# A two-layer encoder trunk on one core: the transposition stages between the layers at each piece of the pass over memory, and eight products of zeros at the head

## The chip, the core and the metric

The kernel runs on one core of a Trainium2 chip. The engines that matter here are TensorE (PE in the profile; its loads of the stationary operand are PEld), VectorE (DVE), ScalarE (ACT), GpSimd (POOL) and SyncE (SP, which issues most of the DMAs). Each has a queue of its own, and they meet at semaphores. The metric is the device time of one execution in microseconds, the median of several runs. The time of the kernel before and the profile of one of its executions are below.

## What is computed

The reference is a trunk of two layers over 256 tokens of width 2048, batch 1. Each layer projects its input once, runs three groups of heads side by side (banded softmax attention, gated linear attention, attention into 256 memory tokens), multiplies each group by a SiLU gate, projects the joined groups and normalizes the residual:

```python
def hybrid_layer(x, mem, w_in, rel_table, gate_w, gate_b, gla_norm_g, w_mem_kv, w_out, ln_g, ln_b):
    h = x @ w_in
    ...
    mkv = mem @ w_mem_kv
    mk, mv = jnp.split(mkv, 2, axis=-1)
    ...
    y = jnp.concatenate([y_a * jax.nn.silu(a_z), y_b * jax.nn.silu(b_z), y_m * jax.nn.silu(m_z)], axis=-1)
    out = y @ w_out
    return layer_norm(DEEPNORM_ALPHA * x + out, ln_g, ln_b)
```

Two things matter for the change. `mem @ w_mem_kv` doesn't depend on the layer's input, so the second layer can start with it while the first layer's output is still being normalized. And the normalized output is the input of the next layer's projection: it is needed with the model's width on the partitions, that is transposed.

## The kernel before

**Products.** All large products are of float32 operands that are split in two parts: a high part (a cast on ACT) and a low part (the rest, a subtraction on DVE), with high x high, high x low and low x high added up in PSUM. The functions high (L189) and low (L202) split each weight load, parts (L340) splits an activation. A load is 128 x 1024 floats, 512 KB. The list of loads is laid out by plan (L128) in the order of use; take (L236) hands the next one to the products and lets advance (L214) issue casts three loads ahead, splits two ahead, and DMAs so that at most four raw loads (RAWS) are held. There are four buffers for high parts and three for low parts. A raw buffer is free for its next DMA when its low part is made.

**Who sets the order.** The instructions of PE and of SP stand in the order in which the program emits them. Those of ACT and DVE are placed by a planner, which simulates a timeline; the casts and splits of weights have a high priority there. So a small step on DVE can stand far ahead of its place in the program.

**Work in the gaps.** Small jobs (heads, the normalization) are generators. They are advanced by tick (L92), which the loops over weights call once behind each piece of products. A generator says with `yield n` after how many ticks it is due again; at most two are active, and a tick advances one of them by one step. finish (L108) ticks until the given ones are done, with no products between:

```python
            after = next(g, None)
            if after is not None:
                active.append((g, now[0] + after))
                return
```

**The pass over memory.** A layer starts with `mem @ w_mem_kv` (L723 to L738): 16 pieces, s=0 to s=15, each with one weight load. Pieces 0, 1, 3, 5, 7, 9, 11 and 13 make values (function moving, L291: 12 products), the others keys (function stationary, L282: 16 products). The memory comes in four quarters, each cast and split into an operand tile. Operand tiles (L163) rotate through five buffers, and the four quarters of the layer's transposed input use the same five. Behind each piece stands a tick. After the pass the key sums are added, cast and split (L739 to L743); the tile for them comes from gated (L85), which has two buffers. Then `finish(gens)` (L745) completes what is left of the normalization, and the group of products for the linear attention's queries and keys follows (L757), the first to read the transposed input. Its first half writes PSUM banks 4 and 5.

**The normalization between the layers.** norm_between (L632) is put on the list at the end of layer 0 (L850), so that its steps fall to the ticks of layer 1's pass over memory. It first makes the statistics and normalizes the residual `res` in place (L637 to L642). Then come eight transposition stages, two for each quarter q of the width (L646 to L661), called stage 0 to stage 7 here. A stage takes one of the PSUM banks 4 and 5, the only ones that are free during the pass, transposes four blocks of 128 x 128 on PE (L655), applies the norm's gain and bias with two activations on ACT into a tile from gated() (L658), gives the bank back, and casts and splits the tile into the operand (L660, by way of L341 and L342). The pauses between the steps are 2 after the first quarter's normalization (L644), 3 after all of it (L645), and the one at the end of a stage (L661).

norm_residual (L663) later multiplies `res` by the gain and adds the bias, for the residual of layer 1 (L667, L668); it comes behind the transposes of the same columns.

**The head.** begin (L251) issues the first loads in small parts, and then products of a tile of zeros (L275, L276) whose result is not used; the first true product writes its bank anew. The number is ZEROS (L32).

Of the kernel before, what the change touches and what calls it, by code (L numbers as in the profile page):

```python
# [28 lines left out]

G_MK, G_MV, G_BQK, G_AQ0, G_AK0, G_AQ1, G_AK1, G_MQ, G_BZ, G_AZ0, G_AZ1, G_MZ, G_WO = range(13)  # L30
HI_AHEAD, LO_AHEAD, RAWS = 3, 2, 4
ZEROS = 7  # L32
FILL = 8
AHEAD = 4000

# [8 lines left out]
def hybrid_trunk_kernel(  # L44
# [27 lines left out]
    def nm(s):  # L72
        uid[0] += 1
        return f"{s}_{uid[0]}"

    def mm(o, l, r, start, stop):
        pe.matmul(o, l, r, start=start, stop=stop, skip_group_check=True)  # L77
# [4 lines left out]
    def small(shape, tag, bufs=1):  # L82
        return sm.tile(shape, F32, name=nm(tag), tag=tag, bufs=bufs)

    def gated():  # L85
        return hd.tile([P, 2, T], F32, name=nm("sz"), tag="sz", bufs=2)
# [27 lines left out]
    def banks(n):  # L114
        while len(free) < n:
            yield 1
        return [free.pop(0) for _ in range(n)]

    def release(*bs):
        free.extend(bs)  # L120
# [42 lines left out]
    def operand():  # L163
        return opp.tile([P, 4, 2, T], F32R, name=nm("x"), tag="x")
# [86 lines left out]
    def begin():  # L251
# [22 lines left out]
        at["dma"] = 3  # L274
        for i in range(ZEROS):  # L275
            mm(ps[:, 2 + i % 2], zero[:, :P], zero, True, True)  # L276
# [63 lines left out]
    def parts(hi, lo, src):  # L340
        act.copy(hi, src)  # L341
        dve.tensor_tensor(lo, src, hi.bitcast(F32), op=ALU.subtract)  # L342

    def rsqrt(dst, src, n, epsc):
        v = small([P, n], f"rs_v{n}", 2)
        u = small([P, n], f"rs_u{n}", 2)
        act.activation(u, src, AF.Sqrt, bias=eps[:, 0:1] if epsc == LN_EPS else eps[:, 1:2])
        dve.tensor_scalar(v, src, epsc, -0.5, op0=ALU.add, op1=ALU.mult)
        dve.reciprocal(dst, u)
        dve.tensor_tensor(u, dst, dst, op=ALU.mult)  # L350
        dve.tensor_tensor(u, u, v, op=ALU.mult)
        dve.scalar_tensor_tensor(dst, u, 1.5, dst, op0=ALU.add, op1=ALU.mult)
# [261 lines left out]
    def columns(n):  # L614
        return slice(n * 512, (n + 1) * 512)
# [16 lines left out]
    def norm_between(x):  # L632

        mvt = small([P, 2, 2], "mvt")
        rstd = small([P, 2], "rstd")
        for t in range(2):
            dve.bn_aggr(mvt[:, t], stats[:, t, :4])  # L637
        rsqrt(rstd, mvt[:, :, 1], 2, LN_EPS)
        for q in range(4):
            for t in range(2):  # L640
                r = res[:, t, columns(q)]
                dve.tensor_scalar(r, r, mvt[:, t, 0:1], rstd[:, t:t + 1], op0=ALU.subtract, op1=ALU.mult)  # L642
            if q == 0:
                yield 2  # L644
        yield 3  # L645
        for q in range(4):  # L646
            o = operand()
            x.append(o)
            for j in range(0, 4, 2):
                pt, = yield from banks(1)  # L650
                z = gated()
                for jj in range(2):
                    kt = q * 4 + j + jj
                    for t in range(2):
                        pe.transpose(ps[:, pt, jj * T + t * P:jj * T + (t + 1) * P], res[:, t, kt * P:(kt + 1) * P], ident)  # L655
                for jj in range(2):
                    kt = q * 4 + j + jj
                    act.activation(z[:, jj], ps[:, pt, jj * T:(jj + 1) * T], AF.Identity, bias=lnt[:, 1, kt:kt + 1], scale=lnt[:, 0, kt:kt + 1])  # L658
                release(pt)
                parts(o[:, j:j + 2, 0], o[:, j:j + 2, 1], z)  # L660
                yield 2 if q < 3 else 1  # L661

    def norm_residual(rows):  # L663
        for n, (g, b) in enumerate(rows):
# [50 lines left out]
    for l in range(L):  # L715
# [7 lines left out]
        for s in range(16):  # L723
# [3 lines left out]
            for kk in range(2):  # L727
                kt = p * 2 + kk
                x, j = memq[l][kt // 4], kt % 4
# [47 lines left out]
        def heads():  # L777
            t = hd.tile([P, 4, T], F32, name=nm("qk"), tag="qk", bufs=4)
            for i, a, b in ws_group(l):
                total(t[:, i:i + 2], a, b)  # L780
            return t
# [17 lines left out]
        for half in range(2):  # L799
            values(2 + half)  # L800
            q, k = heads(), heads()
            gens.append([a_head(half * 4 + h, load_bias, bias, q[:, h], k[:, h], asv, yraw[1 + half][:, h]) for h in range(4)])
            waiting.extend(gens[-1])
        q = [hd.tile([P, 4, T], F32R, name=nm("mq"), tag="qk", bufs=4) for _ in range(2)]
# [44 lines left out]
        if not last:  # L849
            gens = [norm_between(xq[l + 1])]  # L850
            waiting.extend(gens)
# [111 lines left out]
```

## Time and profile before

| What | Value |
|---|---|
| Median of 3 runs | 947.04 us |
| Lowest and highest | 946.37 and 947.05 us |
| The profiled execution | 945.37 us |
| Its span, first to last instruction | 943.6 us |
| Mean granted clock of TensorE | 0.993 |
| Moved by DMA | 178.72 MB, mean 189 GB/s |

The profile is of one execution. In its views a row of a timeline has the start in us from the span's start, the busy time, the engine, the line, the operation, the tiles written and read, the shape, how many instructions are merged, and in brackets how long the engine was idle before it and what ended that. A line can be a helper's: L77 is the one function through which nearly all products go, L207 and L200 make the parts of weights, L341 and L342 those of activations. The granted clock is a share of full speed.

### The profile page before, as it was taken

The numbers are of one execution on the slowest core, as the hardware profiler recorded it, in microseconds if no ns is written. First come the engines' busy times: TensorE is split into PE (matmuls) and PEld (weight loads), VectorE is DVE, ScalarE is ACT, GpSimd is POOL, SyncE is SP. The second block draws the span as 40 slices with busy tenths as digits, with TensorE's granted clock in tenths as the row PEclk, the third lists the DMA queues.
The fourth block names the chain that finished last, engine by engine and source line by source line (L and its number), as shares of the span: only waits on it lengthen the run. The fifth ranks groups of instructions, "written<-read, shape, count | busy, mean of one in ns | idle before, by whom it ended". The sixth has DMA issues, their size and how long they took to land.

```text
span 943.6 us, 14238 instructions
## 1 busy us (share of the span) xinstructions
PE 925.7 (98%) x5529; PEld 812.7 (86%) x5529; DVE 588.0 (62%) x779; ACT 502.4 (53%) x721; POOL 16.5 (2%) x38
## 2 busy tenths in 40 slices
PE   8999999999999999999996999999999999999997
PEld 6889998998888888888885899989988888888875
DVE  5674497565566666655688444975655666666566
ACT  5554484474456665443466345755744566654340
POOL 1000000000000010000000000000000000100000
PEclk9999999999999999999998899999999999999999
DMA  8868665555545476655665366654655545665552
GB/s 290 295 197 277 207 202 163 156 175 186 195 157 171 162 221 208 197 191 192 217 205 179 107 178 205 200 164 138 197 183 181 175 157 187 209 207 195 191 172 89
DMA packets 58451, 178.72 MB, mean 189 GB/s; under 512 B 6352, under 2 KB 9488, under 8 KB 58128
## 3 DMA queue, kind: packets, MB, share of 16 engines
q1 hardware_dynamic: 56560, 173.05, 56.3%
q0 software_dynamic: 1536, 4.24, 2.0%
q8 instruction: 43, 0.70, 0.3%
q10 hardware_dynamic: 288, 0.52, 0.2%
q14 instruction: 24, 0.20, 0.1%
HBM read 175.70 MB, written 2.10 MB: 188 GB/s over the span
## 4 chain that ended last, share of the span: by engine, by line
PE 93%; DVE 3%; DMA 2%; issue 1%; ACT 1%; SPq 0%; ACTq 0%; DVEq 0%
PE ps L77 91%; DVE wl L207 1%; DMA room<-w 1%; DMA raw<-w 1%; DMA raw<-memT 1%; PE ps L559 1%; PE ps L597 0%; DVE res L642 0%; DVE res L667 0%; PE ps L655 0%; SPq L272 0%; ACT sz L658 0%; DVE w L207 0%; PE ps L528 0%; SPq L267 0%
## 5 line engine op out<-in xcount | busy, mean ns | idle before, releaser
L207 DVE TENSOR_TENSOR wl<-raw,wh 128x1024 fp32r<-128x1024 f32 (+1 forms) x313 | 366.0, 1171 | 280.7 <-PE ps L77 217.2
L200 ACT CAST wh<-raw 128x1024 fp32r<-128x1024 f32 (+1 forms) x313 | 314.9, 1007 | 333.7 <-PE ps L77 233.6
L77 PE MATMUL ps<-x,wh 128*128 128x512 f32 x1408 | 450.9, 401 | 7.9 <-ACT sz L658 7.7
L77 PEld LDWEIGHTS ps<-x,wl 128*128 128x128 f32 x1408 | 265.3, 188 | 63.4 <-DVE wl L207 1.0
L77 PE MATMUL ps<-wh,x 128*128 128x512 f32 (+1 forms) x1112 | 318.8, 368 | 0.6 <-ACT wh L278 0.6
L77 PE MATMUL ps<-x,wl 128*128 128x256 f32 x1408 | 278.1, 279 | 0.5 <-DVE wl L207 0.5
L77 PEld LDWEIGHTS ps<-x,wh 128*128 128x128 f32 x1408 | 217.5, 190 | 10.8 <-ACT sz L658 8.5
L77 PEld LDWEIGHTS ps<-wh,x 128*128 128x128 f32 x1112 | 204.2, 188 | 24.8 <-ACT wh L278 2.0
L77 PE MATMUL ps<-wl,x 128*128 128x512 f32 (+1 forms) x556 | 204.2, 367 | 1.1 <-DVE wl L207 1.1
L77 PEld LDWEIGHTS ps<-wl,x 128*128 128x128 f32 x556 | 104.3, 188 | 14.8 <-DVE wl L207 2.0
L550 ACT ACTIVATE sc<-sc,mx 128x128 f32<-128x128 f32 (+1 forms) x32 | 14.3, 448 | 19.8 <-DVE mx L548 19.8
L338 DVE SCALAR_TENSOR_TENSOR sz<-ps,sz 128x512 f32<-128x512 f32 x24 | 16.5, 690 | 2.3 <-ACT sz L337 0.3
L619 DVE SCALAR_TENSOR_TENSOR res<-res,ps 128x512 f32<-128x512 f32 x16 | 10.9, 684 | 8.0 <-PE ps L77 8.0
L337 ACT ACTIVATE sz<-ps 128x512 f32<-128x512 f32 x24 | 14.2, 592 | 2.0 <-DVE x L342 1.8
L77 PE MATMUL ps<-w,x 128*128 128x512 f32 (+1 forms) x72 | 14.3, 357 | 0.0
L77 PEld LDWEIGHTS ps<-w,x 128*128 128x128 f32 x72 | 12.0, 189 | 2.2
L406 ACT ACTIVATE sc<-sc 128x512 f32<-128x512 f32 x12 | 7.6, 633 | 11.3 <-DVE sc L404 11.3
L831 DVE TENSOR_TENSOR yr<-sz,yr 128x512 f32<-128x512 f32 x16 | 11.0, 687 | 4.2 <-ACT sz L829 4.2
L829 ACT ACTIVATE sz<-sz 128x512 f32<-128x512 f32 x16 | 10.1, 632 | 6.1 <-DVE sz L338 6.0
L77 PE MATMUL ps<-qk,qk 128*128 128x128 f32 (+1 forms) x64 | 13.1, 327 | 0.0
L77 PE MATMUL ps<-sc,asv 128*128 128x256 f32 (+1 forms) x64 | 13.0, 326 | 0.0
L342 DVE TENSOR_TENSOR x<-yr,x 128x512 fp32r<-128x512 f32 x16 | 10.7, 688 | 3.2 <-ACT x L341 3.1
(171 smaller groups left out, 514.4 us busy)
## 6 DMA issues: line engine op xcount, KB each, us to landing
raw<-w SPq DMA_DIRECT2D x252, 512.0 KB, 3.7
raw<-w SPq DMA_DIRECT2D x64, 388.0 KB, 3.1
bias<-relw SPq DMA_DIRECT2D x16, 192.0 KB, 3.8
res<-xT SPq DMA_DIRECT2D x4, 512.0 KB, 5.8
res<-xn SPq DMA_DIRECT2D x1, 2048.0 KB, 8.2
sc<-ln_g POOLq DMA_DIRECT2D x8, 256.0 KB, 4.4
sc<-ln_b POOLq DMA_DIRECT2D x8, 256.0 KB, 5.9
raw<-memT SPq DMA_DIRECT2D x4, 512.0 KB, 4.8
```

The costliest lines, as they stand in the source:

```text
L77: pe.matmul(o, l, r, start=start, stop=stop, skip_group_check=True)
L200: act.copy(d.hi, d.raw)
L207: dve.tensor_tensor(d.lo, d.raw, d.hi.bitcast(F32), op=ALU.subtract)
L337: act.mul(dst, b, scale)
L338: dve.scalar_tensor_tensor(dst, a, scale, dst, op0=ALU.mult, op1=ALU.add)
L342: dve.tensor_tensor(lo, src, hi.bitcast(F32), op=ALU.subtract)
L406: act.activation(dd, dd, AF.Abs)
L550: act.activation(s[:, own[t]], s[:, own[t]], AF.Exp, bias=mx[:, t:t + 1], accum_out=zs[:, t:t + 1])
L559: pe.transpose(ps[:, pt, i * P:(i + 1) * P], s[:, i * P:(i + 1) * P], ident)
L619: dve.scalar_tensor_tensor(r, r, ALPHA, acc, op0=ALU.mult, op1=ALU.add)
L829: act.activation(sz, sz, AF.Silu)
L831: dve.tensor_tensor(yraw[i][:, j:j + 2], sz, yraw[i][:, j:j + 2], op=ALU.mult)
```

## The change

Two edits. The pause at the end of a transposition stage was 2 ticks for the first three quarters and 1 for the last; it is now 1 tick everywhere, except after the stage (q, j) = (2, 2), the last of the third quarter, where it is 2. And the number of products of zeros at the head goes from 7 to 8.

```diff
-ZEROS = 7
+ZEROS = 8
...
                 release(pt)
                 parts(o[:, j:j + 2, 0], o[:, j:j + 2, 1], z)
-                yield 2 if q < 3 else 1
+                yield 2 if (q, j) == (2, 2) else 1
```

What is computed stays the same.

## The prediction

> **What bounds the kernel now.** I read the page first: who is busy, the granted clock, the chain.
>
> ```profile
> PE 925.7 (98%) x5529; PEld 812.7 (86%) x5529; DVE 588.0 (62%) x779; ACT 502.4 (53%) x721; POOL 16.5 (2%) x38
> PEclk9999999999999999999998899999999999999999
> PE 93%; DVE 3%; DMA 2%; issue 1%; ACT 1%; SPq 0%; ACTq 0%; DVEq 0%
> ```
>
> TensorE (PE) sets the time: busy for 98%, and 93% of the chain. What a change can win is an idle gap of PE, or a stretch at a lower clock; PEclk shows one, slices 22 and 23. So the waits of PE come next: engine and line, what it waited for, us in total, times, longest.
>
> ```profile
> PE ps L77 <- ACT sz L658: 7.7, 2, 6.0
> PE ps L77 <- DVE wl L207: 1.7, 3, 0.6
> ```
>
> Nearly all of it hangs on L658, the gain-and-bias activations of norm_between. The timeline of PE around slices 22 and 23, then a stretch of it (us, busy time and count, clock, DMA):
>
> ```profile
> 506.12 0.63 PE L77 MATMUL ps<-x,wh 128*128 128x512 f32 x2
> ...
> 508.92 1.03 PE L655 MATMUL ps<-ident,res 128*128 128x128 f32 x8
> 510.90 0.66 PE L655 MATMUL ps<-ident,res 128*128 128x128 f32 x4 [0.95 <-ACT sz L658]
> 517.58 0.80 PE L77 MATMUL ps<-x,wh 128*128 128x512 f32 x1 [6.03 <-ACT sz L658]
> 520.07 0.80 PE L77 MATMUL ps<-x,wh 128*128 128x512 f32 x1 [1.69 <-ACT sz L658]
> ...
> 524.48 0.62 PE L77 MATMUL ps<-x,wh 128*128 128x512 f32 x2
> ```
> ```profile
> 517.00:524.40 7.40, 5.13 (x16) 0.53 0.00 0
> ```
>
> Piece s=15, the last of the pass over layer 1's memory, runs from 506.12 to 508.92: 16 products in 2.80 us. Then come the last three of the eight transposition stages (8 and 4 transposes), with waits of 0.95, 6.03 and 1.69 us, and the first 16 products of the next group (the stretch's x16) end only at 524.48, at a granted clock of 0.53. Why 6 us? The other engines between:
>
> ```profile
> 512.12 0.68 DVE L338 SCALAR_TENSOR_TENSOR sz<-ps,sz 128x512 f32<-128x512 f32 x1
> 515.73 0.68 DVE L342 TENSOR_TENSOR mk<-sz,mk 128x512 fp32r<-128x512 f32 x1
> 516.51 1.02 ACT L658 ACTIVATE sz<-ps,lnt 128x256 f32<-128x256 f32 x2 [0.67 <-DVE mk L342]
> 518.99 1.02 ACT L658 ACTIVATE sz<-ps,lnt 128x256 f32<-128x256 f32 x2 [0.30 <-DVE x L342]
> ```
>
> The stages of the last quarter (q=3) run in finish(gens), behind the two key sums of L739 to L743. Both take their tile from gated(), which has two buffers. So stage 7's activations wait until the key sum has been added, cast and split (512.12 to 516.41), and the next product group, which writes banks 4 and 5 (first=4), waits until those activations have emptied the banks.
>
> **The change part by part.** First, the order. norm_between starts at the tick of s=0 and pauses 2 and 3, so its first stage falls to the tick of s=5, before and after. Before, with a pause of 2 the next fall to s=7, 9, 11, 13, 15, and two are left to finish(gens). After, with 1 they fall to s=5, 6, 7, 8, 9, 10; (2,2) pauses 2; the last two fall to s=12 and s=13. finish(gens) then finds nothing to do. The pause serves a buffer: the operand of q=3 takes over that of the memory's third quarter, last read by PE in s=12. The operand of q=2 takes over the second quarter's, last read in s=8, and is wanted at s=9. So neither adds a wait on PE beyond program order.
>
> Second, what a stage costs PE wherever it stands:
>
> ```profile
> 478.98 0.60 PE L655 MATMUL ps<-ident,res 128*128 128x128 f32 x4
> 479.33 0.71 PE L77 MATMUL ps<-x,wh 128*128 128x512 f32 x2
> ...
> 482.20 0.63 PE L77 MATMUL ps<-wh,x 128*128 128x512 f32 x2
> ...
> 484.96 0.60 PE L655 MATMUL ps<-ident,res 128*128 128x128 f32 x4
> 485.31 0.71 PE L77 MATMUL ps<-x,wh 128*128 128x512 f32 x2
> ```
>
> Four transposes take 0.35 us (484.96 to 485.31), and the piece behind them 2.87 us (479.33 to 482.20) against 2.80 for s=15: together 0.42. Three more stages ahead of 508.92 move the end of s=15 to 508.92 + 3 x 0.42 = 510.18. The next 16 products at full pace end at 510.18 + 2.80 = 512.98, instead of 524.48. **Gross gain: 11.50 us**: the three waits (8.67), and the rest the slow clock. Does it reach the end? The waits of PE from 520 us on (its first row, the 1.7 at 520.07, left out), and of all engines:
>
> ```profile
> PE ps L77 <- DVE wl L207: 0.5, 1, 0.5
> PE ps L77 <- ACT row L683: 0.3, 1, 0.3
> ```
> ```profile
> ACT wh L200 <- PE ps L77: 233.6, 157, 3.8
> ```
>
> Past the 1.7 that goes, PE loses 0.8 us more, and the casts ahead of it wait mostly for PE itself. So all of it should arrive.
>
> Third, what the denser stages cost. The stretch from s=5 to s=13 has spare time, but not everywhere. The casts of weights from 476 to 509 us as a group (count, busy us, mean ns, idle before), then the timelines of ScalarE (ACT) and VectorE (DVE):
>
> ```profile
> L200 ACT CAST wh<-raw 128x1024 fp32r<-128x1024 f32 x13 | 13.6, 1049 | 12.3 <-DMA raw<-w 9.5 <-PE ps L77 2.8
> ```
> ```profile
> 483.20 1.05 ACT L200 CAST wh<-raw 128x1024 fp32r<-128x1024 f32 x1 [1.06 <-DMA raw<-w]
> 484.15 1.01 ACT L658 ACTIVATE sz<-ps,lnt 128x256 f32<-128x256 f32 x2
> 485.72 1.04 ACT L200 CAST wh<-raw 128x1024 fp32r<-128x1024 f32 x1
> ```
> ```profile
> 485.85 0.69 DVE L342 TENSOR_TENSOR x<-sz,x 128x512 fp32r<-128x512 f32 x1 [0.34 <-ACT x L341]
> 488.89 1.22 DVE L207 TENSOR_TENSOR wl<-raw,wh 128x1024 fp32r<-128x1024 f32 x1
> ```
>
> A stage takes ACT from 484.15 to 485.72, 1.57 us, and DVE 0.69. It issues no DMA. From 484.15 on ACT has eight stages (12.6), the casts of the seven later loads of the pass (the fourth memory quarter among them) and of the first of the next group (8 x 0.95 = 7.6, by the start-to-start times), and the values' cast (about 1, as large as the weights' at 1049 ns): 21.2 us, done at 505.3 if it never waits. PE needs banks 4 and 5 at 510.18: 4.9 us of slack. ACT waited 9.5 us for weight DMAs here; much of the added 4.7 us (three stages) falls into such waits, and that is its cover. DVE gets 3 x 0.69 = 2.1 us.
>
> The exposed place is the start. The first stage's transposes ended at 479.58 (the row at 478.98); its activations started at 484.15, behind a cast that waited for its DMA: ACT took its queue in order. The stage of s=6 now stands behind it, ahead of casts that fed DVE splits with little to spare: the one at 488.89 ends at 490.1, and PE uses it in s=10, two pieces and a stage after 485.31, about 491.3: 1.2 us. A stage put ahead of those casts delays them by 1.57 us and PE by only 0.42; against the 1.2 that is just even (1.57 - 0.42 - 1.2 = -0.05), so some tenths may show in one or two places. The same holds for the third stage, which may find its bank still full. I bound this new waiting from below at -0.62 (the weight wait of PE just ahead of the first stage, shown below, disappears) and from above at 3 x 1.57 = 4.7, three stages' ACT work wholly on the path. **I take 1.0**, nearest to the 0.95 us bank wait, the only wait of that kind shown. If the DMA waits that hide ACT's work were gone, it would be the 4.7.
>
> A rule speaks against packing stages so closely. The Trainium skill, page "TensorE: Matmul & The Clock Gate", section "A second HAM failure mode: psum-queue depth-cycling", reports a kernel that cycled through PSUM banks, idled briefly between groups of products and had its clock go up and down. By it the sum would be that of the last rival below. Here the trace speaks against it for gaps under 1 us: the stretch with a 0.62 wait keeps clock 1.00, as does all of s=6 to s=13 (us, busy of PE, PEld, DVE, ACT, POOL, clock, DMA), and only the 6.03 wait is followed by 0.53.
>
> ```profile
> 476.59 0.50 PE L77 MATMUL ps<-wl,x 128*128 128x512 f32 x1 [0.62 <-DVE wl L207]
> ```
> ```profile
> 476.00:479.00 3.00, 2.41 (x11) 1.96 (x12) 3.00 (x4) 0.64 (x1) 0.00 (x0) 1.00 0.39 116
> 478.98:502.90 23.92, 23.92 (x130) 20.33 (x129) 17.93 (x22) 16.19 (x23) 0.64 (x2) 1.00 0.76 248
> ```
>
> Fourth, the eighth product of zeros.
>
> ```profile
> 1.51 3.35 PE L77 MATMUL ps<-wh 128*128 128x512 f32 x7 [1.51 <-DVE wh L248]
> 4.83 0.84 PE L77 MATMUL ps<-wh,x 128*128 128x512 f32 x2
> 7.22 0.73 PE L77 MATMUL ps<-wh,x 128*128 128x512 f32 x2 [0.62 <-ACT wh L278]
> ```
>
> Seven take 3.35 us; taking one's 0.80 (the row at 517.58) for the last leaves (3.35 - 0.80) / 6 = 0.43 start to start. The eighth starts at about 4.49, and the first true product moves from 4.83 to 4.92 at most. 0.62 us of waiting at 7.22 for a cast behind a DMA covers that, and covers equally what the first products might gain by a better clock. I take 0; without the cover it would cost 0.1 to 0.43.
>
> **Sum.** 11.5 - 1.0 - 0 = 10.5 us. The profiled execution took 945.37 us, 943.6 of it span; by it the time would be 934.9. It lies 1.67 below the median of the runs, 947.04, which is what is predicted: 947.04 - 10.5 = **936.5 us**.
>
> **The rivals.**
> *ACT and the raw buffers fall behind* (0.14). Four raw buffers are refilled only after DVE's split, so a late stage delays a cast, the split, the next DMA. For it: those DMA waits of 9.5 us. Against: 4.9 us of slack at the end. Price 4.7: 947.04 - 11.5 + 4.7 = 940.2.
> *The group still waits* (0.05): the last stage's activations, queued behind the values' cast and the key sums, release bank 5 late. It takes over 4.9 us of lag; I price it at half of the 6.03 wait: 936.5 + 3.0 = 939.5.
> *No change* (0.02): the wait at 517.58 belongs to something other than these stages, and comes back whole: 947. Against: both activations end just ahead of both products (517.53, 520.01).
> *Slower* (0.04): the bank waits repeat at every stage and the clock falls as it did after 517. Place: s=6 to s=13, 23.92 us and three stages, 25.2 us. At 0.53 they take 25.2 x (1/0.53 - 1) = 22.3 us more: 947.04 - 11.5 + 22.3 = 957.8. It decides from half of the stretch on (11.5 us). For it: two stages back to back cost 0.95. Against: a bank is now wanted again only two pieces, 5.6 us, later.
>
> **How the numbers follow.** The forecast, 0.75, covers 934.3 (947.04 - 11.5 - 0.62 and some half us of measurement) to 939. The first rival reaches past 940.2; range 934.3 to 941.0. A measurement of this kernel tells about 0.2% from no change, 1.9 us, so the first three cases are faster: 0.94, less 0.01 for a tail of the first rival. Faster 0.93, same 0.03, slower 0.04.
>
> **What would show it.** Right: the 7.7 of PE on L658 gone or under 1.5; transposes after s=5, 6, 7, 8, 9, 10, 12, 13; the next group's products right behind s=15 at clock 1.00; slices 22 and 23 at 9; PE busy nearer 99%. ACT's waits for weight DMAs in the pass shorter by some us. Wrong: new PE waits on wl L207, wh L200 or L658 at L655 between 482 and 505 us that sum to over 3 us; a clock below 0.9 there; a wait in front of the second half of the next group, for the key sums; a start moved by more than 0.2 us at 12 us.

## The result, and the profile after

The changed kernel took 933.83 us (median of 4 runs, 933.71 to 934.99), the kernel before 946.7 us (median of 4 runs in the same comparison, 945.1 to 947.05). The ratio, of the means of these runs, is 0.987, with a 95% interval of 0.9853 to 0.9887. The forecast was 936.5 us in a range of 934.3 to 941.0. The sign and the cause were right. The gain was larger than forecast: 933.83 itself lies half a microsecond below the range, and the ratio applied to the 947.04 us that the prediction started from gives 934.7, just inside it.

The page after the change, in the parts that were shown of before: the busy times, the granted clock by slice, the chain.

```profile
PE 923.4 (99%) x5530; PEld 812.0 (87%) x5530; DVE 587.3 (63%) x779; ACT 502.0 (54%) x721; POOL 16.5 (2%) x38
PEclk9999999999999999999999999999999999999999
PE 96%; DMA 1%; DVE 1%; SPq 0%; issue 0%; ACT 0%; ACTq 0%; DVEq 0%
```

PE's busy time hardly moved (925.7 to 923.4 us), but the span fell from 943.6 to 931.9: what went is idle time and a stretch at low clock. Slices 22 and 23 of the clock are at 9. The waits of PE (what it waited for, us in total, times, longest):

```profile
PE ps L77 <- DVE wl L207: 1.6, 3, 0.7
PE ps L77 <- DVE wh L248: 1.5, 1, 1.5
PE ps L77 <- ACT row L683: 0.3, 1, 0.3
```

The 7.7 us for L658 and the 0.9 us at L655 are gone, and nothing took their place. The timeline of PE around the end of the pass, and two stretches of it (us, busy times with counts, clock, DMA):

```profile
503.83 0.60 PE L655 MATMUL ps<-ident,res 128*128 128x128 f32 x4
504.19 0.71 PE L77 MATMUL ps<-x,wh 128*128 128x512 f32 x2
...
509.85 0.63 PE L77 MATMUL ps<-x,wh 128*128 128x512 f32 x2
...
512.63 0.63 PE L77 MATMUL ps<-x,wh 128*128 128x512 f32 x2
```
```profile
478.50:503.80 25.30, 25.30 (x141) 21.68 (x140) 21.33 (x27) 20.48 (x31) 0.64 (x2) 1.00 0.69 218
503.80:520.00 16.20, 16.20 (x95) 14.17 (x94) 15.29 (x19) 11.04 (x15) 0.00 (x0) 1.00 0.70 199
```

The last stage's transposes stand behind s=13 (503.83). Piece s=15 ends at 509.85, the next group follows without a gap, and its first 16 products end at 512.63 where they ended at 524.48. From the first stage to the next group PE is busy for all of both stretches, at clock 1.00, while ACT is busy for 20.48 of 25.30 us (81%).

To compare kernels without the head of the program, whose length differs a little from one execution to the next, I use one length below: **the pass**, from the start of the first stage's transposes (L655) to the start of the next transposes at L372, some way into layer 1's projections. Before and after:

```profile
580.03 0.38 PE L372 MATMUL ps<-ident,asv 128*16 128x128 f32 x2
```
```profile
478.54 0.60 PE L655 MATMUL ps<-ident,res 128*128 128x128 f32 x4
...
568.17 0.38 PE L372 MATMUL ps<-ident,asv 128*16 128x128 f32 x2
```

Before it was 580.03 - 478.98 = 101.05 us, after 568.17 - 478.54 = 89.63: **11.42 us less, where the prediction's gross gain was 11.50**. The 0.44 us by which 478.54 is earlier than 478.98 come from the head and from one wait ahead of the first stage, and other executions of these kernels have them the other way.

### The profile page after: what moved, and what is told of

It reads as the page before. It is cut to its first block, busy times and chain, and to the rows that moved or that the text cites. A ratio compares the mean times of both kernels' runs of the same rounds, so it can differ in the third digit from the quotient of the medians.

```text
span 931.9 us, 14245 instructions
## 1 busy us (share of the span) xinstructions
PE 923.4 (99%) x5530; PEld 812.0 (87%) x5530; DVE 587.3 (63%) x779; ACT 502.0 (54%) x721; POOL 16.5 (2%) x38
## 4 chain that ended last, share of the span: by engine, by line
PE 96%; DMA 1%; DVE 1%; SPq 0%; issue 0%; ACT 0%; ACTq 0%; DVEq 0%
PE ps L77 95%; DMA room<-w 1%; DMA raw<-w 1%; PE ps L559 1%; DVE wl L207 0%; PE ps L655 0%; PE ps L597 0%; SPq L272 0%; PE ps L528 0%; SPq L267 0%; ACT res L687 0%; ACT wh L200 0%; PE ps L435 0%; DVE res L619 0%; PE ps L372 0%
## 5 line engine op out<-in xcount | busy, mean ns | idle before, releaser
L342 DVE TENSOR_TENSOR x<-yr,x 128x512 fp32r<-128x512 f32 x16 | 10.7, 688 | 3.2 <-ACT x L341 3.1
```

## The experiments

All runs, with the length of the pass in the profiled execution, worked out as above. Each ratio is to runs of the kernel before that stood beside that run (medians of 945.6 to 946.7 us), not to the 947.04 of the first line:

```
kernel                pass us   median us (range, runs)        ratio to before (95%)
before                 101.05   947.04 (946.37-947.05, 3)      1
after                   89.63   933.83 (933.71-934.99, 4)      0.987  (0.9853-0.9887)
after_again             89.64   934.00 (933.48-935.07, 4)      0.9868 (0.9851-0.9885)
pauses_only             89.69   933.75 (933.20-933.90, 4)      0.9871 (0.9858-0.9885)
zeros_only             100.91   945.33 (943.73-946.84, 11)     0.9995 (0.9987-1.0004)
one_left                99.54   944.19 (942.33-945.20, 10)     0.9979 (0.9970-0.9988)
finish_first            96.41   941.75 (940.07-942.81, 4)      0.9955 (0.9941-0.9969)
finish_no_rows          94.94   939.61 (938.97-940.66, 4)      0.9933 (0.9916-0.9949)
act_one_more            90.40   936.80 (935.68-937.49, 4)      0.9902 (0.9887-0.9917)
act_one_more_again      91.37   935.93 (935.02-936.09, 4)      0.9885 (0.9865-0.9904)
act_double              92.60   938.94 (938.39-940.45, 4)      0.9928 (0.9914-0.9943)
one_bank                94.66   938.25 (937.38-939.01, 4)      0.9918 (0.9904-0.9933)
late_start              89.63   934.60 (934.37-935.14, 4)      0.9874 (0.9857-0.9890)
```

**Each edit alone.** pauses_only:

```diff
-                yield 2 if q < 3 else 1
+                yield 2 if (q, j) == (2, 2) else 1
```

> Only the pauses of the change; seven products of zeros as before. Theory (the whole gain is that no stage is left behind the pass): the same time as the changed kernel, 933.5 to 934.3 us, and a ratio to before of 0.986 to 0.988. Rival (the eighth product of zeros brings a part of it, since the changed profile is 0.2 us ahead at 12 us): 934.3 to 934.8, at least 0.3 us slower than the changed kernel.

It took 933.75 us, and its pass is as long as the changed kernel's (89.69): the theory held. As far as these runs can tell, the pauses are the whole gain. zeros_only:

```diff
-ZEROS = 7
+ZEROS = 8
```

> Only the eighth product of zeros. Theory (the head waits for its first loads and casts, so the product is covered): ratio 0.9995 to 1.0005, within 0.5 us of before. Rival (a better clock of the first products): 0.2 to 0.5 us faster. Other rival (the product delays the first true ones and this isn't made good): 0.1 to 0.43 us slower.

The ratio 0.9995 (0.9987 to 1.0004) holds 1: no effect that can be measured. The median is 0.57 us under the 945.9 of before beside it, a hair outside the half microsecond that I had given, but inside the interval, which is too wide to shut out the rival of 0.2 to 0.5 us faster. The head shows why such a number says little. The first product of whole-load size, with its 128x512 `x,wh`, starts in this kernel and in pauses_only (seven zeros) at:

```profile
13.04 0.73 PE L77 MATMUL ps<-x,wh 128*128 128x512 f32 x2 [0.29 <-ACT wh L200]
```
```profile
12.95 0.73 PE L77 MATMUL ps<-x,wh 128*128 128x512 f32 x2 [0.66 <-ACT wh L200]
```

In both it waits for a cast, a wait of the kind that the prediction took for its cover. With eight zeros the changed kernel had 12.21 here, with seven the kernel before 12.43: the point moves by 0.8 us between executions, and not with the number of zeros.

**What the stages waited for.** one_left leaves a single stage behind the pass:

```diff
-                yield 2 if q < 3 else 1
+                yield 2 if q < 2 else 1
```

> Pause 2 in the first two quarters, 1 in the last two, from the kernel before: stages behind s=5, 7, 9, 11, 13, 14, 15 and one left to finish(gens). Theory (the stage that is left waits for the tile of the first key sum, so one stage left costs most of what two cost): 941.5 to 945.5 us, PE waiting about 4 to 6 us for L658. Rival (each stage left behind the pass costs its own share, so one left keeps over half of the gain): 937 to 940.5 us.

The theory held. With one stage left the time is 944.19 us and the pass is shortened by only 1.51 us. PE's waits sum to 6.8 us, above the 4 to 6 expected, in one of 0.95 and one of 5.83. The row of PE's wait, and ACT's at its end:

```profile
PE ps L77 <- ACT sz L658: 6.8, 2, 5.8
```
```profile
516.75 1.02 ACT L658 ACTIVATE sz<-ps,lnt 128x256 f32<-128x256 f32 x2 [1.27 <-DVE mk L342]
```

The last stage's activations waited until DVE had split the first key sum, whose tile they take. So the one stage that is left waits 5.83 us here, where the first of two waited 6.03.

finish_first keeps both stages behind the pass and puts them ahead of the key sums:

```diff
-        for i in range(2):
-            tmp = gated()
...
         if l:
             finish(gens)
             waiting.append(norm_residual(rows))
+        for i in range(2):
+            tmp = gated()
...
```

> The kernel before, with finish(gens) moved ahead of the two key sums; pauses as before, two stages still left behind the pass. Theory (the key sums hold the tiles of the last two stages; the rest of the wait is that stage 5's split stands behind six rows of residual work on DVE, which frees stage 7's tile at about 514.5 us): 940 to 943 us. Rival A (the key sums are all of it): 936 to 939. Rival B (the wait is the stages' own run through ACT, whatever stands ahead): 945 to 947.

941.75 us, and a pass of 96.41: the key sums were a part of the wait, worth 101.05 - 96.41 = 4.64 us of the pass. A part of what was left stands in DVE's timeline:

```profile
509.90 1.29 DVE L667 TENSOR_TENSOR res<-res,sc 128x512 f32<-128x512 f32 x2
511.10 0.68 DVE L668 TENSOR_TENSOR res<-res,sc 128x512 f32<-128x512 f32 x1
511.71 1.29 DVE L667 TENSOR_TENSOR res<-res,sc 128x512 f32<-128x512 f32 x2
512.91 0.69 DVE L668 TENSOR_TENSOR res<-res,sc 128x512 f32<-128x512 f32 x1
513.51 0.68 DVE L342 TENSOR_TENSOR x<-sz,x 128x512 fp32r<-128x512 f32 x1
```

The split of stage 5 frees the tile for stage 7, and the planner had put six rows of the residual's gain and bias ahead of it. In the kernel before, six such rows stand ahead of that split too, from 510.32 to 514.52. finish_no_rows leaves those out:

```diff
             finish(gens)
-            waiting.append(norm_residual(rows))
```

> As finish_first, and norm_residual is left out: the sixteen gain and bias products on the residual of layer 1 (L667, L668) are not computed, so its output is another one. Theory (in finish_first the last stage waited for stage 5's split, 513.51 us on DVE, behind four of these rows): that split starts at about 511.8 us, PE's wait of 3.46 us for L658 falls to about 1.7, its clock has no time to fall, and the time is 937.5 to 939 us, some 3.4 under finish_first. Rival (the rows are not in the way, the wait is ACT's): within 0.8 us of finish_first's 941.75.

The theory held for the wait, not for the time. The split moved from right behind the residual rows to right behind its cast, and PE's last wait fell from 3.46 to 1.85 us. The splits on DVE, then PE and its clock:

```profile
513.04 1.29 DVE L342 TENSOR_TENSOR x<-sz,x 128x512 fp32r<-128x512 f32 x2 [1.90 <-ACT x L341]
```
```profile
511.64 0.66 PE L655 MATMUL ps<-ident,res 128*128 128x128 f32 x4 [0.95 <-ACT sz L658]
512.55 0.50 PE L77 MATMUL ps<-x,wh 128*128 128x512 f32 x1 [0.26 <-ACT sz L658]
514.90 0.66 PE L77 MATMUL ps<-x,wh 128*128 128x512 f32 x1 [1.85 <-ACT sz L658]
```
```profile
514.90:518.30 3.40, 3.40 (x11) 2.91 (x12) 2.58 (x4) 2.14 (x4) 0.00 (x0) 0.53 0.01 5
```

But the time is 939.61 us, above the expected 937.5 to 939, because the clock fell all the same: 0.53 for 3.4 us, which costs about 1.6. The longest single gap was 1.85 us; three gaps of 0.95, 0.26 and 1.85 us lay within 4.2 us (510.7 to 514.9).

With the key sums and the rows both out of the way the pass is still 94.94 - 89.63 = 5.31 us longer than the changed kernel's. The three gaps (3.06 us) and the slow clock (1.6) are most of that: it is the price of two stages behind the pass by themselves, through their two banks, two tile buffers and ACT. A third buffer for the tile, which would test the tile alone, was not run.

**Whether the dense stages have room.** act_one_more and act_double give ACT more to do in every stage of the changed kernel:

```diff
-                for jj in range(2):
+                for jj in (0, 0, 1):
                     kt = q * 4 + j + jj
                     act.activation(z[:, jj], ...
```

act_double has `(0, 1, 0, 1)` in the same place.

> The changed kernel with one activation of each stage issued twice on the same data: 8 x 0.5 = 4.2 us more for ACT in the pass, the same result. Theory (ACT's work is covered: it was done with stage 7's banks 2.8 us early and had 1.8 us of waits): 933.8 to 934.8 us, PE's new waits under 1 us. Rival (the dense stages are at ACT's limit, as my 1.0 us of new waiting supposed): 936 to 938 us.

> The changed kernel with both activations of each stage issued twice: 8 x 1.04 = 8.3 us more for ACT, the same result. Theory (4.6 us of slack, and what exceeds it stands on the path): 8.3 - 4.6 = 3.7 us, so 936.5 to 938.5 us, in waits of PE for banks at L655 and for the first products of the next group, at clock 1.00. Rival (ACT far from the bound): 933.8 to 934.8. Rival (repeated waits pull the clock down): over 945 us and a granted clock under 0.9 between 480 and 515 us.

act_one_more took 936.8 us. By its time the rival held; by its profile the theory, for the pass was only 0.77 us longer. The profiled execution was the fastest of the four (935.68 us). So it ran again beside the changed kernel:

> The changed kernel with one activation of each stage issued twice, once more. Its first profile showed only 0.8 us of new waiting in the pass, its median 3 us. Theory (the waiting of the profile, and the rest was other waits of those executions): 0.5 to 1.5 us above the changed kernel beside it. Rival (ACT at its limit costs in most executions more than in the profiled one): 2.2 to 3.5 us above it.

> The changed kernel once more, beside the next two on one chip. Theory: 933.3 to 934.6 us, a spread of about 1 us, against over 2 us for before, whose clock recovers at a different point of each execution. Rival (the first comparison caught lucky runs): 935 to 937 us.

The changed kernel repeated its time (934.0 us). act_one_more_again took 935.93, 1.93 us more, between the two ranges, and now its profile agrees: the pass is 1.73 us longer than beside it. So the theory, which let ACT's slack of 4.6 us swallow nearly all of 4.2, was too kind. The place of the waits tells why:

```profile
485.78 0.66 PE L655 MATMUL ps<-ident,res 128*128 128x128 f32 x4 [0.49 <-ACT sz L658]
...
496.47 0.66 PE L655 MATMUL ps<-ident,res 128*128 128x128 f32 x4 [0.79 <-ACT sz L658]
```

They are the third and the sixth stage, each waiting for the bank of the stage two before it. In the changed kernel the third stage's first weight load (PEld) already waited 0.15 us for it, while products were still running, so PE lost nothing:

```profile
483.80 1.02 ACT L658 ACTIVATE sz<-ps,lnt 128x256 f32<-128x256 f32 x2
...
484.87 0.47 PEld L655 LDWEIGHTS ps<-ident,res 128*128 128x128 f32 x4 [0.15 <-ACT sz L658]
484.99 0.60 PE L655 MATMUL ps<-ident,res 128*128 128x128 f32 x4
```

The activations were over at 484.82, 0.17 us before the transposes at 484.99. The slack over the whole pass was there, but at this stage there was next to none. act_double, at 938.94 us, lies just above its range; its pass grew by 2.97 us, most of it in three waits (0.27 and 0.79 us for banks, 1.09 us for the split of a memory quarter), at clock 1.00. The slow clock that one rival expected didn't come.

**Whether waits for banks pull the clock down.** one_bank:

```diff
-            free[:] = [4, 5]
+            free[:] = [4]
```

> The changed kernel with one PSUM bank for the stages instead of two (free = [4]); the orders of ACT and DVE are the same. Theory (only the second stage comes too early for one bank: its transposes at 481.8 us against the first stage's activations, done at 484.8): one wait of PE of 3.0 us and small ones, clock near 1.00, 936 to 938.5 us. Rival (PE waits at every stage and its clock falls, as the last rival of the prediction had it): over 945 us. Rival (one bank is enough): under 934.5 us.

The theory held for the time, 938.25 us, and for the single wait, but not for the clock, which it had near 1.00. PE's timeline there and the clock behind it:

```profile
485.19 1.03 PE L655 MATMUL ps<-ident,res 128*128 128x128 f32 x4 [3.22 <-ACT sz L658]
```
```profile
485.00:491.00 6.00, 5.81 (x23) 4.84 (x24) 4.42 (x7) 4.23 (x8) 0.00 (x0) 0.72 0.48 165
```

The pass is 94.66 - 89.63 = 5.03 us longer: 3.22 of waiting, and 1.8 of slow clock until about 488.6. After that no stage waited, at one bank. So the second bank is worth 5 us of this pass (4.4 by the medians), at the start alone, where ACT's queue stands behind a late cast.

**Fewer stages at the start.** late_start, from the changed kernel:

```diff
-                yield 2 if (q, j) == (2, 2) else 1
+                yield 2 if q < 1 else 1
```

> The changed kernel with pause 2 in the first quarter and 1 afterwards: stages behind s=5, 7, 9, 10, 11, 12, 13, 14. Theory (PE waits for no stage in the changed kernel, so thinning them at the start wins nothing; the last stage has one piece, 2.8 us, until its bank is wanted, and its activations took 2.9 us from transposes to release): within 0.5 us of the changed kernel. Rival (the dense start costs): 0.5 to 1 us faster. Rival (the last stage comes too late): 0.5 to 2 us slower, in a wait for L658 behind s=15.

The pass is 89.63 us to the hundredth, and 934.6 us is 0.6 above the changed kernel beside it, with ranges that overlap: a tenth outside the half microsecond of the theory, but without the wait for L658 that the slower rival needs. In these two placements there is nothing to win in where the stages stand, as long as none is left behind. No version beat the changed kernel by more than the noise.

## Why the prediction was right

**The cause.** The stages behind the pass waited, the wait was the last to end there, and moving them into the pass removed it. pauses_only and the lengths of the pass show it, one_left that a stage left behind brings nearly all of it back. The prediction's account of the 6.03 us was right in kind but not complete: of the 11.42 us, having the key sums ahead cost 4.64, six residual rows ahead of a split on DVE another 96.41 - 94.94 = 1.47, and two stages behind the pass cost the remaining 5.31 by themselves. The prediction did not name the rows. It also put the wait on the wrong stage: the activations that start at 516.51, behind the first key sum's split, are stage 6's; stage 7's are those at 518.99, behind another split (x, L342).

**The gross gain.** 11.50 us by the three waits, the slow clock and 0.42 us of PE for each stage; 11.42 was measured. From the first stage to the end of s=15 five stages took 508.92 - 478.98 = 29.94 us before and eight take 509.85 - 478.54 = 31.31 after, so a further stage cost 1.37 / 3 = 0.46 us, nearly as taken.

**The term that was mis-sized: "I take 1.0", the new waiting of the dense stages.** It measured 0.0: PE was busy for the whole stretch. The place was right, the size not. The third stage was the exposed one, and it cleared by 0.17 us, so that nothing showed there is in part luck. The other exposed place, the split that PE uses in s=10, didn't come, because the planner wrote a new order: it put the memory quarter's cast and split behind three stages, and that weight's split before it. In DVE's timeline after the change they are 4 us apart, in the other order than before:

```profile
488.64 1.22 DVE L207 TENSOR_TENSOR wl<-raw,wh 128x1024 fp32r<-128x1024 f32 x1
...
492.90 1.22 DVE L207 TENSOR_TENSOR x<-raw,x 128x1024 fp32r<-128x1024 f32 x1
```

I had taken the old order of DVE and pushed it back. The other end of that range, 4.7, was not reached even with 8.3 us more on ACT, which cost 2.97 in the pass.

**The cover.** The three stages' work on ACT was to fall into its waits for weight DMAs. It did for the most part; the row of the casts from 476 to 509 us is now:

```profile
L200 ACT CAST wh<-raw 128x1024 fp32r<-128x1024 f32 x11 | 11.5, 1049 | 7.5 <-DMA raw<-w 6.2 <-PE ps L655 1.3
```

The waits for DMAs fell from 9.5 to 6.2 us, and 6.0 of these 6.2 come before the first stage's activations at 483.80. So 3.3 of the added 4.7 us went there, and behind that start this cover is all but used up. The slack at the end, 4.9 us by the prediction, came out as 2.8 us left and 1.8 of waits.

**The step from the profile to the median.** The prediction carried the 1.67 us between the profiled execution and the median of before over to the changed kernel. There the two agree: 933.71 profiled, 933.83 median. The forecast by the profile was 934.9, and 1.2 above the profile's 933.71; the forecast by the median was 2.7 above. The kernel before varies more: 944.55 to 947.87 us in 21 runs beside the first four experiments, against 933.2 to 935.07 us for the twelve runs of after, after_again and pauses_only. The wider range is in part that of more runs. What differs is the stretch behind the gap, an obvious place for such a spread; no profile of a long run was taken, so that is argued and not shown.

**The zeros.** Cost and gain of nothing that can be measured, as taken.

**The rivals.** ACT and the raw buffers: not in the changed kernel; waits of PE for stages came with more work on ACT (act_one_more, act_double) or with one bank. The group still waits: no; stage 7's activations, 506.03 to 507.06 on ACT, had its bank free 2.8 us before 509.85. No change: no. Slower by a falling clock: the Trainium skill's page "TensorE: Matmul & The Clock Gate", section "A second HAM failure mode: psum-queue depth-cycling", tells of a clock that goes up and down when a kernel cycles through banks with short idle times between. In this kernel the banks were cycled through eight times in 25 us and the clock stayed at 1.00, while PE was never idle; with one bank it fell once, behind the one gap of 3.22 us.

## What to carry to other kernels

Work that another engine must finish before a matrix engine can go on belongs between products, not behind the last of them: here one piece left behind cost 99.54 - 89.63 = 9.91 of the 11.42 us. Count the buffers that such a step shares with what stands beside it in the program: here a two-buffer tile tied a transposition to a sum that no product was waiting for yet. Room on a helper engine is to be counted at each step, not only in total: the margin was 4.6 us over the pass and 0.17 us at the third stage.

## What was not expected of the hardware

The clock fell without a gap longer than 1.85 us: in finish_no_rows three gaps of 0.95, 0.26 and 1.85 us within 4.2 us were followed by 3.4 us at 0.53, and in one_bank one gap of 3.22 us by about as long. Single gaps of 0.5 to 1.1 us, two of them some 10 us apart in act_one_more_again and two within 2.8 us (0.79 and 1.09) in act_double, left it at 1.00. The Trainium skill's page "TensorE: Matmul & The Clock Gate", section "What's actually happening", gives an idle window of about 3.4 us, free-running, as the condition. The 3.22 us are near it; the three gaps, with four transposes (0.66 us) and one product (0.50 us) between them, don't fit a window that has to be idle throughout. Whether such short work counts there, no run here shows.
